# Branch A's query blocks and the output stage's pairs taken from last to first

## The chip, the cores and the metric

The kernel runs on one core of a Trainium2 chip. The metric is the device time of one execution in microseconds (us), taken on that core; lower is better. The engines are called as the profile calls them: PE (TensorE, with PEld for its weight loads), DVE (VectorE), ACT (ScalarE), POOL (GpSimd) and SP (the queue that issues every DMA of this kernel).

## The reference

One layer over 2048 tokens of width 1024. A layer norm and one wide input projection feed three branches. Branch A is sparse attention: an indexer scores all keys, each query keeps the best 256 that its 64-token chunk limit allows, and eight heads of width 64 attend to one shared key and value head. Branch B is differential attention, branch C attends to 256 memory tokens. Each branch is gated, projected to 1024 and merged; an output projection and a second layer norm end the layer.

```
h = _layer_norm(x, ln_in_g, ln_in_b)
proj = h @ w_in[l]
...
o_a = _dsa_attention(a_q, a_k, a_v, i_q, i_k, i_w).reshape(bsz, seq, A_WIDTH)
y_a = (o_a * jax.nn.silu(a_gate)) @ w_proj_a[l]
...
merged = g[:, :, 0] * y_a + g[:, :, 1] * y_b + g[:, :, 2] * y_c
h = _layer_norm(DEEPNORM_ALPHA * h + merged @ w_out[l], ln_g[l], ln_b[l])
```

Block b of branch A holds the 128 queries from token 128b on and looks at the first (b+1)*128 keys, so its work grows with b from 1 unit to 16 units of 128 keys.

## The kernel before

The 2048 tokens are 16 blocks of 128, or 8 pairs of 256. Products in float32 are made of two halves (a rounded high part and the rest), so most projections are three matmuls (`mm3`, L72 to L74). What one stage leaves for another goes through DRAM: `oa_d[b]` (branch A's result of a block), `ob_d[b]`, `mg_d[p]` (the merged sum of a pair), `tm_d`, `sg_d` (the gates), `bias_d[b]` (which keys a query of block b keeps).

A scheduler turns the program into one fixed list of instructions for each engine: an instruction goes where its operands are expected to be ready, and among those that are ready the one written first is preferred. So stages that are written one after the other are interleaved. The text below concerns the last 1000 us, in which these run beside each other:

- `attn_a(b)` (L736 to L794), branch A. For two heads at a time (a "chain" below, four for each block): the logits `lg` on PE in pieces of 512 keys (L623, L624), their eviction to `AP` on DVE (L626), the row minimum `anm` (L766), the exponential on ACT in pieces of 1024 keys (L769), then for each 256 keys a transposition `apt` on PE (L777), the split into two halves `apr` on ACT and DVE (L66, L69) and the products `aops` on PE (L782). `os`, `ot` and `ao` collect a block, which is stored to `oa_d[b]` (L794). The bias of a block has one buffer. The blocks run in an order that is written out by hand: 7, 0, 6, 1, 5, 2, 4, 3, then 8 to 15.
- `dense_g(1)`, the last of the input projection (`dps`), still under way when branch A begins.
- the loop over the pairs of branches B and C (L911 to L923): transpositions and small attention in `cps`, projections in `yps`, and the merged sum stored to `mg_d[p]` (L923). Its weights `w_proj_b` and `w_proj_c` are loaded and split first (L822, ACT L66, DVE L69, tiles `whP`).
- `stage1(p)` (L933 to L944): the gated result of branch A of a pair (`fo`, transposed in `gT`) is projected with `w_proj_a` (`yps` again, 4 pieces of 24 matmuls), multiplied by its gate `ft` on DVE (L845) and added to the sum read back from `mg_d[p]` in `facc` (L944).
- the loop over the first `EARLY` = 4 pairs (L950 to L958): `stage1`, and the sum back to `mg_d[p]` (L954). After the second of them all of `w_out` is loaded, 16 pieces of 256 KB, each split into tiles `whP` and `wwo`. These pieces and the sums take their buffers from one ring of three, named `facc`:

```
acc = accs(fs, 3)
stage1(p, acc)
...
wo += load_w(fw, fs, "facc", w_out, 4, ("wo2", "wo3"), 3)
```

- `ready(p)` (L972 to L985) fetches the sum of a pair (from DRAM for the early ones, through `stage1` for the others) and splits it into `fmT`; `stage2(b)` (L987 to L1007) multiplies by `w_out` (`fz`, PE), adds `h` and does the last layer norm. The buffers of these two lie where branch A's were, so they are free when branch A's last block is stored. The last block that runs has its norm cut finer.

Of the kernel before, what the change touches and what calls it, by code (L numbers as in the profile page):

```python
# [22 lines left out]
NB = S // 128  # L23
NP = NB // 2
# [10 lines left out]
GV = 3  # L35
AHEAD = 1
EARLY = 4
WO = (1, 1)
YT = 8
YO = 1  # L40
# [13 lines left out]
def tile_layer(ctx, tc, x, mem, ln_in_g, ln_in_b, w_in, w_mem_kv, diff_lambda, diff_norm_g,  # L54
# [589 lines left out]
    for hd in range(4):  # L644
# [25 lines left out]
        for b in order:  # L670
# [8 lines left out]
            for c in range(2):  # L679
                if b < 8 and c == 1:  # L680
                    p = both[:, 1]
                elif b < 8:
                    both = bp.tile([128, 2, 1024], F32, name="P", bufs=PB)
                    p = both[:, 0]
                else:
                    p = bp.tile([128, S], F32, name="P", bufs=PB)
# [106 lines left out]
            V.tensor_tensor(oo, oo, rc[:, 4 * h4:4 * h4 + 4, None].to_broadcast([128, 4, 64]), op=ALU.mult)  # L793
        SP.dma_start(oa_d[b], o.rearrange("p h d -> p (h d)"))  # L794

    for b in [7, 0, 6, 1, 5, 2, 4, 3, 8, 9, 10, 11, 12, 13, 14, 15]:
        attn_a(b)

    dense_g(1)
# [146 lines left out]
    def accs(ap, bufs):  # L946
        return [ap.tile([128, 2, 256], F32, name="facc", bufs=bufs) for _ in range(4)]

    wo = []
    for p in range(EARLY):  # L950
        acc = accs(fs, 3)
        stage1(p, acc)
        for u in range(4):
            SP.dma_start(mg_d[p][:, 2 * u:2 * u + 2], acc[u])  # L954
        if p == WO[0]:
            wo += load_w(hTp, fs, "facc", w_out, 0, ("hP2", "hP3"), 3)
        if p == WO[1]:
            wo += load_w(fw, fs, "facc", w_out, 4, ("wo2", "wo3"), 3)  # L958

    aps.release()  # L960
# [8 lines left out]

    MT = {}  # L970

    def ready(p):  # L972
        if p >= NP:
            return
        acc = accs(fp, 4)
        if p < EARLY:
            for u in range(4):
                SP.dma_start(acc[u], mg_d[p][:, 2 * u:2 * u + 2])
        else:
            stage1(p, acc)  # L980
        MT[p] = fp.tile([128, 2, KT, 256], F32R, name="fmT", bufs=AHEAD + 1)
        for u in range(4):
            H, L = (MT[p][:, a, 2 * u:2 * u + 2] for a in range(2))
            A.activation(H, acc[u], AF.Copy, scale=0.5)
            V.scalar_tensor_tensor(L, acc[u], 0.5, H.bitcast(F32), op0=ALU.mult, op1=ALU.subtract)  # L985

    def stage2(b):  # L987
        hh = fp.tile([128, D], F32, name="fh", bufs=3)
        SP.dma_start(hh, h_d[b])
        mT = MT[b // 2][:, :, :, 128 * (b % 2):128 * (b % 2) + 128]  # L990
        nz = 4 if b == NB - 1 else 2
        for n in range(nz):
            c = slice(n * (D // nz), (n + 1) * (D // nz))
            z = fq.tile([128, 512], F32, name="fz")[:, :D // nz]
            for k in range(KT):
                mm3(z, mT[:, 0, k], mT[:, 1, k], wo[k][:, 0, c], wo[k][:, 1, c], k == 0, k == KT - 1)
            V.scalar_tensor_tensor(hh[:, c], hh[:, c], ALPHA, z, op0=ALU.mult, op1=ALU.add)
        mu, rs = norm_stats(fp, hh, nz)
        if b < NB - 1:
            V.tensor_scalar(hh, hh, mu, rs, op0=ALU.subtract, op1=ALU.mult)  # L1000
            G.tensor_tensor(hh, hh, gln, op=ALU.mult)
            V.tensor_tensor(hh, hh, bln, op=ALU.add)
            SP.dma_start(out[b * 128:(b + 1) * 128, :], hh)
            return
        for c in (slice(0, 512), slice(512, 1024)):
            V.scalar_tensor_tensor(hh[:, c], hh[:, c], mu, gln[:, c], op0=ALU.subtract, op1=ALU.mult)
            V.scalar_tensor_tensor(hh[:, c], hh[:, c], rs, bln[:, c], op0=ALU.mult, op1=ALU.add)  # L1007
            SP.dma_start(out[b * 128:(b + 1) * 128, c], hh[:, c])

    for p in range(AHEAD):  # L1010
        ready(p)
    for p in range(NP):
        ready(p + AHEAD)
        stage2(2 * p)
        stage2(2 * p + 1)
    fq.release()
    fp.release()
    fqr.release()
# [52 lines left out]
```

## Time and profile before

| | us |
|---|---|
| median of 3 runs | 2973.35 (2971.82 to 2976.17) |
| span of the profiled execution, first to last instruction | 2965.9 |
| PE busy, PEld busy, share of the span | 95%, 92% |
| DVE, ACT, POOL busy, share of the span | 77%, 49%, 33% |
| bytes moved by DMA | 379.47 MB, mean 128 GB/s |

The runs are timed by the device around the whole execution; the span of the profile leaves out what lies before the first and behind the last instruction. The profiled execution has no time of its own in the list of runs: beside its span of 2965.9 us the median is 7.45 us longer and the fastest run 5.9 us longer. In a timeline a row gives the start, the duration, and behind the shape how many instructions of a kind are merged; what the engine waited for stands in brackets. Matmuls overlap, so the time that one costs is the distance between two starts, not its duration.

### The profile page before, as it was taken

What the parts mean: (1) busy time and instruction counts of PE and PEld (TensorE: products, weight loads), DVE (VectorE), ACT (ScalarE), POOL (GpSimd) and SP (SyncE); (2) the same over time, 40 slices, a digit from 0 to 9 for tenths busy, and PEclk for the clock granted to TensorE, in tenths of its full rate; (3) what the DMA queues carried; (4) which work ended last, traced back from release to release, by engine and by line L of the source; (5) the groups of instructions that cost most, each with busy time, mean ns of one, the idle gap of its engine ahead of it and who ended that gap; (6) DMA issues with size and microseconds to landing.
All of it is one profiled execution on the core that took longest, in us unless ns stands there. A gap on an engine that the chain in (4) does not pass through costs nothing. (4 is left out here: it accounts for less than half of the span.)

```text
span 2965.9 us, 57460 instructions
## 1 busy us (share of the span) xinstructions
PE 2830.5 (95%) x21616; PEld 2715.7 (92%) x21616; DVE 2279.2 (77%) x5309; ACT 1442.6 (49%) x2806; POOL 983.2 (33%) x1064
## 2 busy tenths in 40 slices
PE   7979998999999998999999999999999999988998
PEld 6979998999999998999999999988999999978887
DVE  6499988999899998676667766658787777776655
ACT  4345673677266772333344334446566556544100
POOL 6663547242522236323324222302222222200221
PEclk9999999999999999999999999999999999999999
DMA  6554434433232234624234242273433333256532
GB/s 208 171 191 138 159 113 156 133 119 114 94 101 76 82 93 147 201 73 140 89 118 142 77 128 80 75 242 110 133 114 119 102 113 102 86 172 224 172 131 79
DMA packets 320949, 379.47 MB, mean 128 GB/s; under 512 B 26400, under 2 KB 236832, under 8 KB 320160
## 3 DMA queue, kind: packets, MB, share of 16 engines
q1 hardware_dynamic: 320672, 375.80, 40.2%
q8 instruction: 171, 2.80, 0.4%
q14 instruction: 106, 0.87, 0.1%
HBM read 236.02 MB, written 139.69 MB: 127 GB/s over the span
## 5 line engine op out<-in xcount | busy, mean ns | idle before, releaser
L72 PE MATMUL dps<-hP,w 128*128 128x256 f32 x2048 | 582.6, 284 | 15.1 <-DVE do L69 9.9
L74 PE MATMUL dps<-hP,w 128*128 128x256 f32 x2048 | 581.7, 284 | 0.0
L73 PE MATMUL dps<-hP,w 128*128 128x256 f32 x2048 | 581.2, 284 | 0.0
L72 PE MATMUL dps<-w,hP 128*128 128x256 f32 (+1 forms) x1664 | 491.1, 296 | 12.5 <-POOL w L64 3.1
L73 PE MATMUL dps<-w,hP 128*128 128x256 f32 (+1 forms) x1664 | 490.0, 295 | 0.0
L74 PE MATMUL dps<-w,hP 128*128 128x256 f32 (+1 forms) x1664 | 487.9, 294 | 0.0
L72 PEld LDWEIGHTS dps<-hP,w 128*128 128x128 f32 x2048 | 392.6, 192 | 21.6 <-DVE do L69 10.7
L74 PEld LDWEIGHTS dps<-hP,w 128*128 128x128 f32 x2048 | 392.5, 192 | 4.4 <-POOL w L69 0.3
L73 PEld LDWEIGHTS dps<-hP,w 128*128 128x128 f32 x2048 | 392.7, 192 | 3.6
L533 ACT ACTIVATE ja<-sall,thr 128x1280 bf16<-128x1280 f32 (+4 forms) x224 | 302.2, 1349 | 122.6 <-DVE thr L529 107.1
L64 POOL TENSOR_SCALAR w<-wr 128x1024 fp32r<-128x1024 f32 x120 | 135.5, 1129 | 629.5 <-PE dps L74 404.9
L72 PEld LDWEIGHTS dps<-w,hP 128*128 128x128 f32 x1664 | 324.0, 195 | 16.8 <-issue 4.3
L69 POOL TENSOR_TENSOR w<-wr,w 128x1024 fp32r<-128x1024 f32 (+1 forms) x128 | 332.1, 2595 | 15.0 <-ACT w L66 6.9
L520 DVE TENSOR_SCALAR_CACHE_REDUCE jd<-sall,thr 128x1408 bf16<-128x1408 f32 (+6 forms) x231 | 330.9, 1433 | 5.9
L73 PEld LDWEIGHTS dps<-w,hP 128*128 128x128 f32 x1664 | 324.3, 195 | 1.8
L74 PEld LDWEIGHTS dps<-w,hP 128*128 128x128 f32 x1664 | 323.8, 195 | 2.2
L691 ACT ACTIVATE P<-P,nm 128x128 f32<-128x128 f32 (+15 forms) x128 | 154.1, 1204 | 197.8 <-DVE nm L690 187.5
L626 DVE CUSTOM_DVE_ANT_0 AP<-lg,bias 128x512 f32<-128x512 f32 (+3 forms) x304 | 181.9, 619 | 68.4 <-PE lg L624 25.1
L66 ACT CAST apr<-apt 128x512 fp32r<-128x512 f32 (+1 forms) x288 | 158.4, 563 | 141.7 <-PE apt L777 108.4
L633 DVE TENSOR_SCALAR_CACHE_REDUCE P<-lg 128x512 f32<-128x512 f32 (+3 forms) x288 | 170.4, 596 | 72.3 <-PE lg L624 71.2
L493 DVE SCALAR_TENSOR_TENSOR sall<-ir,iw,sall 128x512 f32<-128x512 f32 (+3 forms) x266 | 217.1, 865 | 8.9 <-ACT ir L489 8.0
L782 PE MATMUL aops<-apr,VA 128*128 128x256 f32 x1088 | 206.7, 297 | 16.8 <-DVE apr L69 6.7
(249 smaller groups left out, 7109.2 us busy)
## 6 DMA issues: line engine op xcount, KB each, us to landing
wr<-in_w_in_dram SPq DMA_DIRECT2D x112, 512.0 KB, 3.9
tm_d<-do SPq DMA_DIRECT2D x96, 256.0 KB, 2.1
bq<-qb_d SPq DMA_DIRECT2D x128, 128.0 KB, 3.1
aq<-qa_d SPq DMA_DIRECT2D x128, 128.0 KB, 3.1
yt<-tm_d SPq DMA_DIRECT2D x64, 256.0 KB, 3.6
sg_d<-do SPq DMA_DIRECT2D x48, 256.0 KB, 2.1
ys<-sg_d SPq DMA_DIRECT2D x48, 256.0 KB, 3.1
facc<-mg_d SPq DMA_DIRECT2D x48, 256.0 KB, 4.1
```

Of the source, the lines that this page charges most:

```text
L66: A.copy(H, src)
L69: el.tensor_tensor(L, src, H.bitcast(F32), op=ALU.subtract)
L72: PE.matmul(ps, lH, rH, start=start, stop=False)
L73: PE.matmul(ps, lH, rL, start=False, stop=False)
L74: PE.matmul(ps, lL, rH, start=False, stop=stop)
L493: V.scalar_tensor_tensor(s[:, c0:c0 + cn], r[:, :cn], iw[:, h:h + 1], s[:, c0:c0 + cn], op0=ALU.mult, op1=ALU.add)
L520: V.tensor_scalar(jd[:, :L], sc[b], t.bitcast(F32)[:, i:i + 1], None, op0=op, op1=ALU.add, accum_out=dst[:, i:i + 1])
L533: A.activation(ja[:, :L], sc[b], AF.Sign, bias=thr.bitcast(F32)[:, i:i + 1], scale=-1.0, accum_out=cnt[:, i:i + 1])
L626: V.tensor_tensor_reduce(P[:, c0:c0 + cn], ps[:, :cn], bias[:, c0:c0 + cn], scale=-0.125, scalar=-LOW, op0=ALU.add, op1=ALU.min, accum_out ...
L633: V.tensor_scalar(P[:, c0:c0 + n0], ps[:, :n0], -0.125, None, op0=ALU.mult, op1=ALU.min, accum_out=mx[:, col, nch:nch + 1])
L691: A.activation(p[:, :L], p[:, :L], AF.Exp, bias=nm[:, c:c + 1], scale=-1.0, accum_out=sm[:, c:c + 1])
L782: PE.matmul(o_ps.rearrange("p a d -> p (a d)"), VA[:, k0 + i], pr[:, a, i].rearrange("p e q -> p (e q)"), start=(k0 + i == 0 and a == 0), ...
```

## The change

Branch A takes its blocks from 15 down to 0. The early loop and the output stage take the pairs in the same order, through a table `PORD` = 7, 6, ..., 0: the first four pairs that get `stage1` early are 7, 6, 5 and 4 in place of 0 to 3, and the last block of the output stage is block 1 in place of 15. The loop of branches B and C still runs from pair 0 to pair 7. No arithmetic is added or removed, and no buffer changes size.

```
+PORD = list(range(NP - 1, -1, -1))
+LAST = 2 * PORD[-1] + 1
...
-    for b in [7, 0, 6, 1, 5, 2, 4, 3, 8, 9, 10, 11, 12, 13, 14, 15]:
+    for b in range(NB - 1, -1, -1):
         attn_a(b)
...
-    for p in range(EARLY):
+    for i in range(EARLY):
+        p = PORD[i]
...
-        if p == WO[0]:
+        if i == WO[0]:
...
-    def ready(p):
-        if p >= NP:
+    def ready(i):
+        if i >= NP:
             return
+        p = PORD[i]
         acc = accs(fp, 4)
-        if p < EARLY:
+        if i < EARLY:
...
-        nz = 4 if b == NB - 1 else 2
+        nz = 4 if b == LAST else 2
...
-        stage2(2 * p)
-        stage2(2 * p + 1)
+        stage2(2 * PORD[p])
+        stage2(2 * PORD[p] + 1)
```

On every engine the lists are the same up to the first instruction that depends on branch A's order. Lines of the new kernel are two to four higher.

**The start of branch A, on PE**, where the last input projections (`dps`) run out. Before, with block 7:

```order
L777 MATMUL apt<-idf,AP 128x128 x6
L623 MATMUL lg<-KA_15284,aq 128x512
L624 MATMUL lg<-KA_15284,aq 128x512
L72 MATMUL dps<-hP_25629,w 128x256
L73 MATMUL dps<-hP_25629,w 128x256
L74 MATMUL dps<-hP_25629,w 128x256
L623 MATMUL lg<-KA_15284,aq 128x512
L624 MATMUL lg<-KA_15284,aq 128x512
L72 MATMUL dps<-hP_25629,w 128x256
L73 MATMUL dps<-hP_25629,w 128x256
L74 MATMUL dps<-hP_25629,w 128x256
L782 MATMUL aops<-apr,VA_15286 128x256 x4
```

Now, with block 15:

```order
L76 MATMUL dps<-hP_25629,w 128x256
L625 MATMUL lg<-KA_15284,aq 128x512
L626 MATMUL lg<-KA_15284,aq 128x512
L625 MATMUL lg<-KA_15284,aq 128x512
L626 MATMUL lg<-KA_15284,aq 128x512
L625 MATMUL lg<-KA_15284,aq 128x512
L626 MATMUL lg<-KA_15284,aq 128x512
L625 MATMUL lg<-KA_15284,aq 128x512
L626 MATMUL lg<-KA_15284,aq 128x512
L779 MATMUL apt<-idf,AP 128x128 x6
```

Eight pieces of logits stand ahead of the first full set of transpositions of block 15, where block 7 had four, and the `dps` have run out by then.

**The end of the early pairs, on DVE**, around the split of the last piece of `w_out` (`wwo`). Before, inside block 15:

```order
L69 TENSOR_TENSOR apr<-apt,apr 128x512
L626 ISA AP,amx<-lg,bias 128x512
L626 ISA amx 128x1
L69 TENSOR_TENSOR wwo_34288<-facc,wwo_34288 128x512 x2
L944 TENSOR_TENSOR facc<-facc,ft 128x512
L766 TENSOR_REDUCE anm<-amx 128x1
L836 SCALAR_TENSOR_TENSOR yoT<-gT,yoT 128x4x128
L69 TENSOR_TENSOR apr<-apt,apr 128x512
L830 TENSOR_TENSOR fo<-fo,ys 128x512
L944 TENSOR_TENSOR facc<-facc,ft 128x512
L69 TENSOR_TENSOR apr<-apt,apr 128x512
L845 SCALAR_TENSOR_TENSOR ft<-ft,yps 128x512
```

Now:

```order
L71 TENSOR_TENSOR wwo_34288<-facc,wwo_34288 128x512
L795 TENSOR_TENSOR ao<-ao,arc 128x256
L71 TENSOR_TENSOR wwo_34288<-facc,wwo_34288 128x512
L832 TENSOR_TENSOR fo<-fo,ys 128x512
L838 SCALAR_TENSOR_TENSOR yoT<-gT,yoT 128x4x128
L946 TENSOR_TENSOR facc<-facc,ft 128x512 x2
L838 SCALAR_TENSOR_TENSOR yoT<-gT,yoT 128x4x128
L832 TENSOR_TENSOR fo<-fo,ys 128x512
L847 SCALAR_TENSOR_TENSOR ft<-ft,yps 128x512 x2
L946 TENSOR_TENSOR facc<-facc,ft 128x512
L989 SCALAR_TENSOR_TENSOR fmT<-facc,fmT 128x512 x4
```

Branch A's last result (`ao`) now stands ahead of the last split, no eviction or split of branch A is left behind it, and the output stage's `fmT` follows at once.

**The same place on SP.** Before (`mg_d_274` is pair 3, the fourth early one, `oa_d_254` block 15, `mg_d_271` pair 0):

```order
L954 DMA mg_d_274<-facc 128x512
L941 DMA ft<-tm_d_4_219 128x512
L829 DMA ys<-sg_d_6_197 128x512
L794 DMA oa_d_254<-ao 128x512
L966 DMA gln<-in_ln_g_dram 128x1024
L968 DMA bln<-in_ln_b_dram 128x1024
L978 DMA facc<-mg_d_271 128x512 x4
```

Now (`mg_d_276` is pair 5, the third early one, `oa_d_239` block 0, `mg_d_278` pair 7):

```order
L944 DMA facc<-mg_d_276 128x512 x2
L796 DMA oa_d_239<-ao 128x512
L944 DMA facc<-mg_d_276 128x512
L939 DMA fo<-oa_d_243 128x512
L831 DMA ys<-sg_d_2_193 128x512
L969 DMA gln<-in_ln_g_dram 128x1024
L943 DMA ft<-tm_d_5_220 128x512 x2
L957 DMA mg_d_276<-facc 128x512 x2
L971 DMA bln<-in_ln_b_dram 128x1024
L982 DMA facc<-mg_d_278 128x512 x4
```

The last store of branch A and the output stage's first loads now stand in the middle of the early pairs, where they stood behind all four.

## Rows read from the trace of the kernel before

**Rows 1.** Busy time by stretch, from the start of branch A on

```profile
core 0: us, PE busy (x) PEld busy (x) DVE busy (x) ACT busy (x) POOL busy (x), PEclk, DMA share, GB/s
1956.00:2010.00 54.00, 46.69 (x325) 42.24 (x324) 39.72 (x113) 34.69 (x78) 4.38 (x4) 0.94 0.83 258
2010.00:2163.00 153.00, 147.60 (x1142) 138.57 (x1141) 121.83 (x394) 94.91 (x244) 36.26 (x36) 1.00 0.47 132
2163.00:2592.00 429.00, 423.51 (x3292) 402.52 (x3291) 323.56 (x879) 256.05 (x588) 103.45 (x103) 1.00 0.34 102
2592.00:2613.60 21.60, 17.85 (x120) 14.73 (x119) 17.48 (x42) 14.37 (x29) 1.65 (x1) 1.00 0.70 230
2613.60:2740.00 126.40, 113.52 (x871) 107.87 (x870) 88.03 (x176) 53.47 (x98) 0.00 (x0) 0.97 0.60 187
2740.00:2958.00 218.00, 218.00 (x1120) 184.41 (x1120) 124.74 (x181) 20.66 (x35) 48.08 (x45) 0.99 0.39 134
...
2740.00:2760.00 20.00, 20.00 (x76) 16.00 (x77) 10.55 (x17) 4.10 (x7) 1.57 (x3) 0.87 0.65 235
```

**Rows 2.** The timeline of PE in places without a wait

```profile
2610.38 0.60 PE L777 MATMUL apt<-idf,AP 128*128 128x128 f32 x4
2610.74 0.48 PE L623 MATMUL lg<-KA,aq 128*128 128x512 f32 x1
...
2618.50 0.28 PE L74 MATMUL yps<-yoT,whP 128*128 128x256 f32 x1
2618.62 0.64 PE L782 MATMUL aops<-apr,VA 128*128 128x256 f32 x4
2619.10 0.38 PE L777 MATMUL apt<-idf,AP 128*128 128x128 f32 x2
...
2628.74 0.39 PE L623 MATMUL lg<-KA,aq 128*128 128x512 f32 x1
2628.97 0.40 PE L624 MATMUL lg<-KA,aq 128*128 128x512 f32 x1
```

**Rows 3.** Groups of PE from 2613.5 to 2739.8: line, operation, count, busy, mean ns, idle

```profile
L73 PE MATMUL yps<-yoT,whP 128*128 128x256 f32 x160 | 46.9, 293 | 0.0
...
L782 PE MATMUL aops<-apr,VA 128*128 128x256 f32 x149 | 29.8, 303 | 8.2 <-ACT apr L66 4.1 <-DVE apr L69 4.0
L777 PE MATMUL apt<-idf,AP 128*128 128x128 f32 x142 | 21.9, 277 | 0.0
```

**Rows 4.** The timeline of SP: the first and the last loads of w_out

```profile
2657.30 0.33 SPq L822 DMA_DIRECT2D facc<-in_w_out_dram  x1
...
2676.99 11.43 SPq L822 DMA_DIRECT2D facc<-in_w_out_dram  x8
```

**Rows 5.** The timeline of DVE in the early pairs

```profile
2648.86 0.68 DVE L845 SCALAR_TENSOR_TENSOR ft<-ft,yps 128x512 f32<-128x512 f32 x1
...
2691.42 1.29 DVE L69 TENSOR_TENSOR wwo<-facc,wwo 128x512 fp32r<-128x512 f32 x2
...
2698.42 0.69 DVE L944 TENSOR_TENSOR facc<-facc,ft 128x512 f32<-128x512 f32 x1 [2.57 <-DMA facc<-mg_d]
...
2699.67 0.69 DVE L845 SCALAR_TENSOR_TENSOR ft<-ft,yps 128x512 f32<-128x512 f32 x1
```

**Rows 6.** The timeline of PE at the end of the w_out loads

```profile
2699.77 0.63 PE L782 MATMUL aops<-apr,VA 128*128 128x256 f32 x3 [3.98 <-DVE apr L69]
...
2700.60 0.44 PE L72 MATMUL yps<-yoT,whP 128*128 128x256 f32 x1
```

**Rows 7.** The start of branch A: DVE, then ACT by form, then PE

```profile
1958.87 0.69 DVE L626 CUSTOM_DVE_ANT_0 AP<-lg,bias 128x512 f32<-128x512 f32 x1 [16.23 <-DMA bias<-bias_d]
1959.49 0.08 DVE L626 DVE_READ_ACCUMULATOR2_ANT amx<- 128x1 f32 x1
...
L769 ACT ACTIVATE AP<-AP,anm 128x1024 f32<-128x1024 f32 x80 | 92.3, 1154 | 26.0 <-DVE anm L766 25.7
...
1999.43 1.11 PE L833 MATMUL cps<-idf,yo 128*128 128x128 f32 x4 [3.54 <-POOL yo L830]
```

More of the change, by code (lines that the diff above doesn't have):

```diff
@@ L954, in tile_layer @@
             SP.dma_start(mg_d[p][:, 2 * u:2 * u + 2], acc[u])
-        if p == WO[0]:
+        if i == WO[0]:
             wo += load_w(hTp, fs, "facc", w_out, 0, ("hP2", "hP3"), 3)
-        if p == WO[1]:
+        if i == WO[1]:
             wo += load_w(fw, fs, "facc", w_out, 4, ("wo2", "wo3"), 3)
@@ L998, in stage2 @@
         mu, rs = norm_stats(fp, hh, nz)
-        if b < NB - 1:
+        if b != LAST:
             V.tensor_scalar(hh, hh, mu, rs, op0=ALU.subtract, op1=ALU.mult)
```

## The prediction

> **What bounds the kernel now.** I read the busy times by stretch first, then the timeline of PE for what each kind of matmul costs, then the timelines of SP, DVE and PE where a stretch loses time. PE bounds nearly all of the last 1000 us: from 2163 to 2592 it is busy for 423.5 of 429 us, and no other engine comes near (DVE 323.6) [rows 1]. The change does not touch that work, it only deals it out anew. So the question is where PE stands still, and whether the new order stands still less. The reader is to see three places in rows 1: the start of branch A (1956 to 2010: PE busy 46.7 of 54 us, granted clock 0.94), the stretch with small blocks of branch A (2010 to 2163), and the stretch of block 15 and the early pairs (2613.6 to 2740: 113.5 of 126.4 us, clock 0.97). From 2740 to 2958 PE never stops.
>
> Matmuls overlap, so I price them from start to start [rows 2]: 0.12 us for 256 columns (`yps`, and `aops` at 0.48 for four), 0.36 for four transpositions, 0.23 for 512 columns of logits. The stretch from 2613.6 to 2740 has 480 `yps` and 149 `aops`, so 75.5 us, 142 `apt` [rows 3] and, counted in the order, 52 other transpositions, 17.5 us, and 46 logits, 10.6 us: 103.6 us of work in 126.4. It loses 22.8.
>
> The Trainium skill (Perfetto Trace Analysis, Identifying the Most-Contended Engine) says that matmul busy time is a poor measure of what is left to gain and weight-load busy time a better one. Here the first leaves 12.9 us and the second 18.5 [rows 1], so by the page more is to be had than the busy row tells; my count of 22.8 goes its way.
>
> **The start of branch A.** Its first two heads need eight evictions and four exponentials before their transpositions can run, where block 7 needed four and two. An eviction takes 0.62 us from start to start and an exponential 1.15 [rows 7], so 4 x 0.62 + 2 x 1.15 = 4.8 us later. The `dps` that covered block 7's first steps are the same number and have run out by then. Against it stands that before, PE waits 3.5 us for the first operands of branch B, with block 7 and the tiny block 0 as its only other work [rows 7], and block 15 has more to put there. The bias of block 15 has twice the bytes of block 7's, and DVE already waited 16.2 us for that one, while PE had `dps` [rows 7]. Ends: 5 us lost, 4 us gained. I take 3 us lost, nearer to the first, because the missing evictions are certain and the wait is one.
>
> **The loop of branches B and C.** Each block has four chains, and each chain begins with a stretch in which only logits can run. With small blocks beside the loop (2010 to 2163, some 28 chains) the weight loads leave 14.4 us open, or 0.5 us for each chain; with big ones (2163 to 2592, also 28) 26.5 us, or 0.95 [rows 1]. Before, 60 chains stand beside the loop (15 blocks); now the loop lasts until the middle of block 3, about 49. Eleven chains at 0.5 to 0.95 are 5 to 10 us. They are not gone, they come back beside the early pairs. Ends: 0, if they lose as much there, and 8 gained, if they lose nothing. I take 3 gained, nearer to 0, because what those early pairs have to offer as cover is itself short of work (next).
>
> **Between the loop and the early pairs** PE has 21.6 us with only branch A, while `w_proj_a` is split and the first gate is formed [rows 1]. The same steps stand there now, with 11.5 us of branch A's work where there were 12.2: 0. The first early pair is now pair 7, whose sum the loop has only just stored, but the sum is wanted some 6 us after the first projection and is loaded well before it; covered by that projection: 0.
>
> **The early pairs.** This is the term that decides. Before, block 15 fills PE while `w_out` comes in; now blocks 2, 1 and 0 are all that is left, and by the order 61.4 us of work stand between the first early projection and the first `fz` (336 `yps`, 56 `aops`, 112 transpositions, 40 narrow logits) in place of 103.6. So 42.2 us of work leave this stretch and are done earlier, beside the loop. If the stretch could shrink by as much, nothing is lost or won. But it holds a chain of its own, the ring of three buffers that the sums and the 16 pieces of `w_out` share:
> - From the first early projection (2613.6) until DVE takes the second piece of the second pair 35.3 us pass [rows 5]. PE's work up to there is 32 us before and 28 to 30 now, so I take 33.
> - From there to the first load of `w_out` 8.4 us [rows 4], the sum being stored and its buffer freed: kept.
> - The 16 loads and splits. Before they run from 2657.3 to 2692 [rows 4, 5], 35 us, the first half held up by branch A's instructions on ACT and DVE. The last eight were issued in 11.4 us, 1.43 each [rows 4]. Sixteen at that pace are 23, and with about 4 for the last one to land and be split 27.
> - From the last split to the next projection of PE, the first of the fourth pair: 2692 to 2700.6, 8.6 us, since DVE first waits for a sum to be read back [rows 5, 6]. Kept.
> - Two pieces of `yps` ahead of the first `fz`, 48 x 0.12 = 5.8.
>
> The sum is 33 + 8.4 + 27 + 8.6 + 5.8 = 82.8 us, and 126.4 - 82.8 = 43.6 us shorter against 42.2 us of work moved out: 1.4 us gained, so 1. The stretch is then no longer full of work, it waits: 82.8 - 61.4 = 21.4 us, as much as it lost before. Ends: with the second piece reached 5 us earlier and loads at 23 us 9 to 10 gained; with 35.3 and 35 us kept 8.6 to 9 lost.
>
> **The output stage** has the same work in pairs and loses nothing [rows 1]; its last block is cut finer as before: 0.
>
> **Sum.** +3 - 3 - 1 = -1 us against the profiled span of 2965.9: 2964.9. The median of the runs is 7.45 us above that span, so **2972 us**. A measurement of this kernel can tell about 0.2% (6 us) from no change.
>
> **Rivals.**
> - *The tail really empties.* The eleven small chains hide wholly in the time in which PE waits for `w_out` anyway (8 gained), the ring starts earlier because PE reaches the second pair sooner and less stands in its way (6 gained), and the start costs nothing. For it: 21 us of waiting are room enough for 11 chains of under 1 us. Against it: the ring starts with the same two pairs, and PE's work ahead of it is hardly less. 14 us off: 2959.
> - *`w_out` loses its cover* (the other side). The place is the ring of early pairs: its loads take 35 us as before and start as late, and PE, in its fixed order, stands before the first projection of the fourth pair with nothing else to do. Price: 2.3 us and 8 us from the two steps of the ring (35.3 for 33, 35 for 27), less the 1.4 gained, so 9; then the clock, which after the waits of this stretch is granted at 0.87 from 2740 to 2760 [rows 1], 2.6 us of lost work, 3 more if the longer wait adds as much again; and the start's 3. In all 15 us: 2988. It decides when more than about 30 us lie between the first and the last load of `w_out`. For it: PE already waited 4.0 us just there, with block 15 at hand [rows 6]. Against it: ACT and DVE have less of branch A between the loads.
>  The Trainium skill (TensorE: Matmul & The Clock Gate, HAM oscillation — how this bites in real kernels) has the rule that speaks against the change: a gap in which PE waits for DMA puts its clock back to half rate, so that the work behind it starts cold. The trace agrees as far as it goes, with 0.87 behind the waits [rows 1]; it would make the price above the rule and not the exception.
> - *The change is not what it says*: the lists show the blocks from 15 to 0 and the pairs from 7 to 0, so this has no chance of its own.
>
> **How the numbers follow.** The forecast, losses that move without changing, has 0.40; the emptied tail 0.35; `w_out` without cover 0.25. The first covers about 2966 to 2979, and the sum's ends reach from 4 + 8 + 10 = 22 gained to 5 + 9 = 14 lost, with 3 to 5 more for the clock. All ends at once are unlikely; leaving out a tenth on each side the range is 2956 to 2988. Faster by over 0.2% is the second case, 0.35, slower the third, 0.25, the same 0.40.
>
> **What would show it.** The first transpositions of block 15 come about 5 us later after the start of branch A than block 7's. The loop of B and C ends later than 2592 by about the work moved, some 20 to 25 us. About 83 us lie between the first projection of the early pairs and the first `fz`, with a wait of PE of 10 us or more, released by DVE, behind the last split of `w_out`, and a lower granted clock after it. I am wrong if that wait is missing (then the tail empties), if the loads of `w_out` take 35 us or more, or if the loop of B and C runs longer than its work.

## The result: 0.95% slower

The changed kernel takes 2999.1 us (median of 4 runs, 2995.0 to 3005.9), the kernel before 2972.6 in the same comparison (2971.6 to 2976.2). The ratio is 1.0095, with a 95% interval of 1.0075 to 1.0114: 26.5 us lost between the medians. The forecast was 2972 and its range ended at 2988. The side was that of the rival in which `w_out` loses its cover, but both the size and the cause are others.

The profiled execution of the changed kernel lasts 3005.85 us, with a span of 3004.1. Its first logits of branch A come 11.9 us later than before (1967.7 against 1955.9), although the lists are identical up to there. The change has no part in this: in the 20 profiled executions of this study that point lies anywhere from 1955.1 to 1967.7. From there to PE's last matmul pass 1002.1 us before and 1028.4 now, 26.3 more, which is nearly the difference of the medians; all that follows is about this part.

The busy time by stretch of the kernel before, cut at the places where the program changes its stage (start of branch A to the first merged sum stored; loop of branches B and C; between; early pairs; output stage). Columns as in [rows 1]:

```profile
core 0: us, PE busy (x) PEld busy (x) DVE busy (x) ACT busy (x) POOL busy (x), PEclk, DMA share, GB/s
1955.86:2073.10 117.24, 107.10 (x777) 97.34 (x776) 93.99 (x301) 77.40 (x187) 16.64 (x17) 0.97 0.60 179
2073.10:2599.00 525.90, 516.64 (x4019) 490.99 (x4018) 397.85 (x1101) 313.27 (x731) 129.07 (x127) 1.00 0.37 111
2599.00:2613.60 14.60, 12.05 (x81) 9.87 (x80) 10.75 (x28) 9.48 (x19) 0.03 (x1) 1.00 0.75 254
2613.60:2739.80 126.20, 113.32 (x871) 107.67 (x869) 87.83 (x176) 53.27 (x98) 0.00 (x0) 0.97 0.60 187
2739.80:2958.00 218.20, 218.20 (x1120) 184.61 (x1120) 124.94 (x181) 20.86 (x35) 48.08 (x45) 0.99 0.39 134
```

The same of the changed kernel, with two rows at its end: 20 us near the end of the early pairs, and a stretch in their middle:

```profile
1967.70:2094.00 126.30, 115.57 (x795) 104.67 (x795) 93.03 (x238) 78.80 (x160) 18.44 (x19) 0.95 0.43 138
2094.00:2651.20 557.20, 541.73 (x4171) 509.16 (x4171) 416.24 (x1132) 325.96 (x744) 126.14 (x125) 1.00 0.35 105
2651.20:2665.80 14.60, 12.95 (x87) 10.15 (x87) 12.44 (x38) 9.89 (x26) 0.00 (x0) 1.00 0.93 268
2665.80:2762.80 97.00, 76.81 (x546) 72.24 (x545) 65.45 (x185) 39.83 (x106) 0.00 (x0) 0.84 0.73 237
2762.80:2996.20 233.40, 233.40 (x1270) 200.34 (x1268) 129.37 (x191) 20.62 (x34) 48.10 (x45) 1.00 0.42 141
2740.00:2760.00 20.00, 9.08 (x42) 7.83 (x43) 11.27 (x19) 5.21 (x9) 0.00 (x0) 0.58 0.91 313
2716.10:2726.40 10.30, 8.85 (x35) 7.28 (x36) 7.56 (x22) 5.22 (x16) 0.00 (x0) 0.50 0.84 265
```

Busy rows hide part of the idling, so I did what the prediction did in one place for the whole stretch: every matmul of PE's timeline is priced from start to start (0.233 us for 512 columns, 0.175 for 384, 0.119 for 256, 0.0875 for 128; [rows 2] show three of these to two digits), and what passes beyond the price is called **loss**. From the first logits of branch A on both traces hold the same 6859 matmuls, so the work so priced is 900.5 us in both kernels. It is only dealt out anew, and the loss is the whole result (the expectations further down name losses from a rougher count, about 2 us lower in the loop):

| us | work before | loss before | work now | loss now |
|---|---|---|---|---|
| start of branch A | 91.9 | 25.3 | 99.5 | 26.7 |
| loop of B and C | 481.6 | 44.4 | 498.0 | 59.2 |
| between | 9.7 | 4.9 | 9.5 | 5.1 |
| early pairs, to the first `fz` | 102.5 | 23.6 | 61.1 | 35.9 |
| output stage | 214.9 | 3.4 | 232.3 | 1.1 |
| all | 900.5 | 101.7 | 900.5 | 128.0 |

Two stages make the difference: the loop loses 14.8 us more, the early pairs 12.3.

**The early pairs.** The three largest waits of PE in this stretch of the changed kernel: engine, what waits, for what, us in total, times, the longest:

```profile
PE gT L835 <- DVE yoT L838: 6.1, 3, 3.0
PE aops L784 <- ACT os L787: 4.4, 1, 4.4
PE gT L835 <- DVE fo L832: 3.8, 1, 3.8
```

From its last 25 us: PE's timeline, the issues on SP, two steps on DVE, and the split of the first sum on ACT:

```profile
2739.87 0.66 PE L790 MATMUL ot<-idf,os 128*128 128x128 f32 x4 [1.49 <-ACT os L787]
2742.96 0.69 PE L835 MATMUL gT<-idf,fo 128*128 128x128 f32 x4 [2.43 <-DVE yoT L838]
2746.63 1.12 PE L835 MATMUL gT<-idf,fo 128*128 128x128 f32 x4 [2.98 <-DVE yoT L838]
2751.59 1.09 PE L835 MATMUL gT<-idf,fo 128*128 128x128 f32 x4 [3.84 <-DVE fo L832]
2754.35 0.55 PE L74 MATMUL yps<-yoT,whP 128*128 128x256 f32 x1 [1.67 <-DVE ft L847]
2754.70 0.42 PE L75 MATMUL yps<-yoT,whP 128*128 128x256 f32 x1
2754.91 0.42 PE L76 MATMUL yps<-yoT,whP 128*128 128x256 f32 x1
```

```profile
2711.63 0.33 SPq L824 DMA_DIRECT2D facc<-in_w_out_dram  x1
...
2736.93 3.70 SPq L824 DMA_DIRECT2D facc<-in_w_out_dram  x3
...
2743.85 0.38 SPq L796 DMA_DIRECT2D oa_d<-ao  x1
...
2750.56 3.19 SPq L982 DMA_DIRECT2D facc<-mg_d  x4
```

```profile
2750.75 0.69 DVE L832 TENSOR_TENSOR fo<-fo,ys 128x512 f32<-128x512 f32 x1 [1.62 <-DMA ys<-sg_d]
2753.51 1.33 DVE L847 SCALAR_TENSOR_TENSOR ft<-ft,yps 128x512 f32<-128x512 f32 x2 [2.07 <-DMA ft<-tm_d]
```

```profile
2758.18 2.49 ACT L988 ACTIVATE fmT<-facc 128x512 fp32r<-128x512 f32 x4 [9.79 <-DMA facc<-mg_d]
```

Block 0, one unit of work, ends branch A at 2743.85; the last piece of `w_out` was issued 3 us earlier; and behind `ot`, PE has only gate transpositions that follow one another through DVE, with nothing between them. Where such steps stand in [rows 6] there are projections or block 15 beside them. DVE is in turn held by loads: 5.3 us of its waits from 2744 to 2754 end with one, the two longest shown above. The clock granted from 2740 to 2760 is 0.58, and the `yps` behind the waits start 0.21 us apart until 2760, where [rows 2] have 0.12. In this stretch it had been 0.50 before, from 2716.1 to 2726.4 and shortly at 2692.

A part of the loss is therefore the clock's. At 0.50 a matmul costs up to about twice its price (projections start 0.21 us apart for 0.12, transpositions at 1988 0.21 for 0.11), so the work done there costs at most its price once more: 3.7 us from 2716.1 on, 4.0 from 2743.4 to 2760.5 and 1.7 at 2692, against 3.2 in two short places of the same stretch before. By this estimate up to 6 of the 12.3 us are the clock's; the other 6 or more are waiting. Before, the first 5 us of the output stage were at half rate too, with 3.0 us of work; now none of it is, which accounts for the 2.3 us by which that stage is better.

**The loop.** Here no wait is long: the longest of PE is 1.7 us. I cut the loop into windows of 4 us and asked how much of each is projections (`yps`). Before, 46 windows have less than 0.8 us of them and lose 25.3 us together; now 54, and they lose 42.8. All other windows lose 17.8 before and 15.6 now. So the extra loss lies where only branch A and the small attention steps of B and C stand. Eight more windows of the old sort (0.55 us each) would be 4.4 us; the greater part is that such a window now loses 0.79. Two stretches of the changed loop show the difference, the first almost without projections:

```profile
2380.00:2400.00 20.00, 17.05 (x113) 13.94 (x111) 14.53 (x41) 12.94 (x32) 4.51 (x5) 1.00 0.28 81
...
2420.00:2440.00 20.00, 20.00 (x161) 19.41 (x160) 14.70 (x42) 13.08 (x35) 4.74 (x6) 1.00 0.40 123
```

And the group of the projections (the first of the three lines of `mm3`) in the one and in the other, 3 against 24:

```profile
L74 PE MATMUL yps<-yoT,whP 128*128 128x256 f32 x3 | 0.9, 316 | 0.0
...
L74 PE MATMUL yps<-yoT,whP 128*128 128x256 f32 x24 | 6.8, 285 | 0.0
```

The waits of PE that the profile shows in the loop grew from 8.5 to 14.4 us, some 6 of the 14.8. What grew are branch A's own steps, logits behind an eviction and products behind a split (before, then now):

```profile
PE lg L623 <- DVE amx L626: 1.2, 3, 0.6
PE aops L782 <- DVE apr L69: 0.9, 3, 0.3
PE aops L782 <- ACT apr L66: 0.7, 2, 0.6
```

```profile
PE lg L625 <- DVE amx L628: 4.0, 6, 1.7
PE aops L784 <- ACT apr L68: 3.1, 5, 1.1
PE aops L784 <- DVE apr L71: 2.3, 8, 0.3
```

The rest is spacing beyond the price that the list of waits does not show. This loss is no chance. The pair of the loop that holds the first of these stretches loses 11.8 us here, and 11.1 to 12.0 in the six other kernels below that share this part of the list.

### The profile page after: what moved, and what is told of

Its sections match the earlier page's. It is cut to its first block, busy times and chain, and to the rows that moved or that the text cites. A ratio compares the mean times of both kernels' runs of the same rounds, so it can differ in the third digit from the quotient of the medians.

```text
span 3004.1 us, 57468 instructions
## 1 busy us (share of the span) xinstructions
PE 2845.0 (95%) x21616; PEld 2723.4 (91%) x21616; DVE 2291.2 (76%) x5309; ACT 1443.2 (48%) x2806; POOL 984.5 (33%) x1064
## 5 line engine op out<-in xcount | busy, mean ns | idle before, releaser
L74 PE MATMUL dps<-w,hP 128*128 128x256 f32 (+1 forms) x1664 | 490.3, 295 | 11.8 <-POOL w L66 3.1
L74 PEld LDWEIGHTS dps<-hP,w 128*128 128x128 f32 x2048 | 392.5, 192 | 27.9 <-DVE do L71 13.5
L71 DVE TENSOR_TENSOR apr<-apt,apr 128x512 fp32r<-128x512 f32 (+1 forms) x288 | 185.0, 656 | 57.2 <-ACT apr L68 55.2
L74 PE MATMUL yps<-yoT,whP 128*128 128x256 f32 x768 | 222.9, 292 | 2.0 <-DVE ft L847 1.7
## 6 DMA issues: line engine op xcount, KB each, us to landing
bq<-qb_d SPq DMA_DIRECT2D x128, 128.0 KB, 3.0
aq<-qa_d SPq DMA_DIRECT2D x128, 128.0 KB, 3.0
```

What stands on the lines that cost most here:

```text
L71: el.tensor_tensor(L, src, H.bitcast(F32), op=ALU.subtract)
L74: PE.matmul(ps, lH, rH, start=start, stop=False)
```

## The experiments

Each run is timed beside the kernel before on its own chip, so the ratios compare. The table has the order of the blocks, the loss by stage worked out as above ("early" with "between"), and the ratio. `alt` stands for 7, 0, 6, 1, 5, 2, 4, 3.

| run | blocks | start | loop | early | output | all | ratio (95%) |
|---|---|---|---|---|---|---|---|
| before | alt, 8 to 15 | 25.3 | 44.4 | 28.5 | 3.4 | 101.7 | 1 |
| changed | 15 to 0 | 26.7 | 59.2 | 41.0 | 1.1 | 128.0 | 1.0095 (1.0075 to 1.0114) |
| e1 | 14 to 0, 15 | 20.4 | 54.5 | 52.6 | 2.6 | 130.2 | 1.0114 (1.0089 to 1.0140) |
| e2 | 7 to 4, 8 to 15, 3 to 0 | 24.2 | 53.3 | 47.7 | 1.1 | 126.3 | 1.0093 (1.0064 to 1.0122) |
| e3 | 15 to 0, ring of 4 | 24.2 | 61.7 | 37.1 | 1.1 | 124.1 | 1.0088 (1.0065 to 1.0112) |
| e4 | 15 to 0, w_out first | 25.1 | 61.0 | 41.2 | 1.0 | 128.3 | 1.0105 (1.0080 to 1.0130) |
| e5 | as before, early pairs 3 to 0 | 24.3 | 43.5 | 25.2 | 2.3 | 95.4 | 1.0001 (0.9987 to 1.0015) |
| e6 | alt, 15 to 8 | 22.3 | 50.7 | 34.0 | 1.1 | 108.1 | 1.0029 (1.0015 to 1.0042) |
| e7 | 0 to 15 | 36.8 | 55.7 | 30.1 | 1.1 | 123.7 | 1.0080 (1.0061 to 1.0099) |
| e8 | as before, ring of 4 | 25.7 | 44.5 | 27.1 | 3.6 | 101.0 | 1.0007 (0.9992 to 1.0023) |
| e9 | 15 to 8, alt | 24.7 | 61.9 | 33.7 | 3.8 | 124.0 | 1.0065 (1.0045 to 1.0086) |
| e10 | 15 to 2 | 24.7 | 60.0 | 24.6 | 12.5 | 121.8 | 1.0038 (1.0025 to 1.0050) |
| e11 | as before without 0, 1 | 21.5 | 51.1 | 31.3 | 1.1 | 105.0 | 0.9987 (0.9971 to 1.0004) |
| e12 | 15, 0, 14, 1 ... 8, 7 | 27.9 | 50.5 | 40.3 | 2.1 | 120.8 | 1.0054 (1.0037 to 1.0070) |
| e13 | 7, 0, 8, 1 ... 13, 6, 14, 15 | 23.6 | 50.1 | 25.1 | 1.1 | 99.8 | 0.9992 (0.9978 to 1.0006) |
| e14 | alt, 14 to 8, 15 | 22.3 | 58.4 | 28.0 | 1.2 | 109.9 | 1.0034 (1.0022 to 1.0047) |
| e15 | 15 to 2, w_out first | 25.3 | 62.1 | 33.8 | 1.4 | 122.6 | 1.0046 (1.0023 to 1.0068) |
| e16 | as before, w_out first | 24.6 | 44.0 | 39.2 | 2.6 | 110.4 | 1.0026 (1.0009 to 1.0042) |
| e17 | 15 to 0, two gate buffers | 25.3 | 59.6 | 44.4 | 1.1 | 130.4 | 1.0097 (1.0071 to 1.0123) |
| e18 | as before, two gate buffers | 27.4 | 43.0 | 33.6 | 3.5 | 107.5 | 1.0016 (1.0002 to 1.0030) |

Work is 900.5 us in all but the runs without blocks 0 and 1 (890.9). The loss is that of one execution and tells the ratio to within some 7 us: the three kernels with the blocks as before and a ratio near 1 (before, e5, e8) have 95 to 102.

### Is it the tail, or the order as such?

e1 puts block 15 last, e2 leaves the loop with ascending blocks and puts only 3 to 0 last.

```
-PORD = list(range(NP - 1, -1, -1))
+PORD = [6, 5, 4, 3, 2, 1, 0, 7]
-    for b in range(NB - 1, -1, -1):
+    for b in [14, 13, 12, 11, 10, 9, 8, 7, 6, 5, 4, 3, 2, 1, 0, 15]:
```

```
-    for b in range(NB - 1, -1, -1):
+    for b in [7, 6, 5, 4, 8, 9, 10, 11, 12, 13, 14, 15, 3, 2, 1, 0]:
```

> Blocks 14 to 0, then block 15 last; pairs 6 to 0, then 7. By the order 45 us of branch A stand again between the first early projection and the first fz (42 in the kernel before, 18 in the changed one), while the loop of branches B and C runs beside descending blocks as in the changed kernel. Theory 'tail' (time is lost where PE has no branch A left while w_out is loaded): PE's loss between first early projection and first fz falls from 35.7 to about 23 us, the loop keeps its 57 us of loss, 2986 us in all, half of the way back. Theory 'all tail' (the loop's extra loss of 14 us is chance of one execution): 2973. Rival 'descending order alone' (blocks that shrink are at fault everywhere): 2995 or more.

> The converse: 7, 6, 5, 4, then 8 to 15 ascending beside the loop, then 3, 2, 1, 0; pairs from 7 to 0. By the order 16 us of branch A stand in the stretch of the early pairs, as few as in the changed kernel (18). Theory 'tail' with a loop of its own cost: the early pairs lose about 36 us as in the changed kernel, the loop about 43 as before, 2986 us in all. Theory 'descending order alone': 2973. Theory 'all tail': 2999.

They contradict each other by these theories. e1 has more of branch A in the early pairs than the kernel before, and still loses more there than the changed kernel (52.6 us with "between", which alone has 14.0 for 4.9); its 1.0114 fits "descending order alone" only. e2 keeps the big blocks ascending and is as slow as the changed kernel, 1.0093, which by its size fits "all tail" only; but its loop loses 53.3 us for 44.4, which that theory has no place for. So a big block at the end is not enough, and ascending big blocks neither. The stores of e2's blocks 15, 3, 2, 1, 0 on SP show what both have in common:

```profile
2642.74 0.38 SPq L796 DMA_DIRECT2D oa_d<-ao  x1
...
2659.98 0.33 SPq L796 DMA_DIRECT2D oa_d<-ao  x1
...
2688.22 1.53 SPq L796 DMA_DIRECT2D oa_d<-ao  x1
...
2710.76 0.33 SPq L796 DMA_DIRECT2D oa_d<-ao  x1
...
2730.25 0.43 SPq L796 DMA_DIRECT2D oa_d<-ao  x1
```

Blocks of 4, 3, 2 and 1 units take 17, 28, 23 and 19 us: from store to store, small blocks next to each other take some 20 us, and not in proportion to their work. In the kernel before the stores of blocks 0 and 1 follow 16.0 and 12.4 us behind those of blocks 7 and 6 (2014.31 to 2030.34, 2058.61 to 2071.05).

### The ring, `w_out` and the gates

e3 and e8 give the ring a fourth buffer, in the changed kernel and in the one before. e4 and e16 load `w_out` one pair earlier. e17 and e18 give the gates of the early pairs two buffers.

```
-        acc = accs(fs, 3)
+        acc = accs(fs, 4)
...
-            wo += load_w(fw, fs, "facc", w_out, 4, ("wo2", "wo3"), 3)
+            wo += load_w(fw, fs, "facc", w_out, 4, ("wo2", "wo3"), 4)
```

```
-WO = (1, 1)
+WO = (0, 0)
```

```
-            gated(fs, fqr, "gT", o, fs.tile([128, 512], F32, name="ys", bufs=1), 0, b, V, oT)
+            gated(fs, fqr, "gT", o, fs.tile([128, 512], F32, name="ys", bufs=2), 0, b, V, oT)
```

> The changed kernel with four buffers in place of three in the ring of the early sums and the raw pieces of w_out. If the ring paces the 16 loads (28.7 us from the first issue to the last) and PE waits for them, the loads take some 20 to 24 us and the kernel gains 4 to 8 us over the changed one: 2991 to 2995. Rival (the splits on ACT and DVE, or the sums ahead of them, set the pace): under 2 us, 2997 to 3000.

> The kernel before with four buffers in the ring of the early sums and w_out. In the changed kernel a fourth buffer took 8 us of loss out of the stretch from the first early projection to the first fz. If the ring holds PE up here as well, the 22.7 us lost in that stretch fall by 3 to 8 and the ratio is 0.997 to 0.999. Rival (block 15 covers the loads, the ring costs nothing): 1.000 within 0.001.

> The changed kernel with w_out loaded behind the first early pair instead of the second. If the stretch is bound by a chain that begins with the first load of w_out (2711.6 in the changed kernel) and PE merely waits at its end, the first load moves some 20 us ahead, into the time of blocks 2 and 1, and 8 to 13 us come back: 2986 to 2991. Rival (what PE lacks is work, wherever the loads stand, since the pairs behind them wait for the same ring): 2997 to 3002.

> The kernel before with w_out loaded behind the first early pair. The prediction took the ring of w_out for what sets the stretch of the early pairs. If that holds here, the wait of 4 us behind the last split goes and the ratio is 0.997 to 0.999. If the small and late steps of branch A set it and the ring is beside them: 1.000 within 0.0015.

> The changed kernel with two buffers in place of one for the gates of the early pairs (ys). In the changed kernel PE waits 9.9 us in that stretch before gate transpositions, and DVE waits for ys up to 1.6 us at a time. If the chain of gates sets the end, the loss between first early projection and first fz falls from 35.7 by 5 to 9 us, ratio to the kernel before 1.006 to 1.008. Rival (small blocks and w_out end as late, the gates only stand in line behind them): 1.009 to 1.0105.

> The same in the kernel before. If the gates' single buffer holds PE there too (it waits 2 to 3.4 us before gate transpositions around the early pairs), the ratio is 0.998 to 0.9995, and this is a version faster than both. Rival (block 15 fills those waits): 1.000 within 0.001.

e3 takes 8 us out of the early pairs (27.6 lost for 35.9) and gives 6 of it back ahead of them (between 9.5 for 5.1, last pair of the loop 11.4 for 9.8); 1.0088 cannot be told from 1.0095. e8 gains nothing. e4 is the test of the prediction's ring. Its first and last `w_out` issues on SP, and its early pairs:

```profile
2676.06 1.86 SPq L824 DMA_DIRECT2D facc<-in_w_out_dram  x2
...
2708.71 1.70 SPq L824 DMA_DIRECT2D facc<-in_w_out_dram  x2
```

```profile
2657.30:2759.20 101.90, 83.65 (x595) 79.10 (x594) 67.03 (x189) 38.15 (x104) 0.00 (x0) 0.88 0.78 244
```

The loads are through 49 us ahead of the first `fz`, where the changed kernel has 22, and nothing is won: 1.0105. In the kernel before the same edit costs 0.26%, all of it in the early pairs. The gates are no cause either: e17 is where the changed kernel is, e18 slightly slower than before. So the rivals of e3, e8 and e17 held; e4's held in its sense, though 1.0105 is some 3004 us and its range ended at 3002; e16 and e18 came out slower than either of their ranges, e18 with an interval that reaches into its rival's. Neither ring nor weights nor gates alone end the stretch, though PE waits for each of them.

One rival is left untested. In e4 DVE waits in the early pairs for the loads that feed a piece:

```profile
DVE ft L847 <- DMA ft<-tm_d: 12.8, 6, 3.4
```

In the changed kernel that row has 2.1 us and the gates' loads 5.7. By the busy times above, the changed stretch moves nearly the bytes that it moved before (237 GB/s for 97.0 us are 23.0 MB, 187 for 126.2 are 23.6) in 29 us less. Whether these loads come late because of the traffic beside them, no run shows.

### The pairs' order

```
+PORD = [3, 2, 1, 0, 4, 5, 6, 7]
```

> The kernel before, with branch A's old order, but the early pairs (and the first pairs of the output stage) taken as 3, 2, 1, 0 in place of 0, 1, 2, 3. It tells what the order of the pairs costs by itself. Theory 'branch A' (the order of the blocks makes the loss, the pairs only follow): the ratio to the kernel before is 1.000 within 0.002. Rival 'pairs' (the sums and gates come back at another time, which stalls the ring): 1.004 or more.

1.0001: taking the early pairs in reverse costs no more than the interval allows, 0.15%. For all eight pairs this wasn't tried, since pairs 7 to 4 can't go first before blocks 8 to 15 are done.

### The order of the blocks, piece by piece

In this order e6, e9, e7, e12, e13 and e14; where no `PORD` stands, e9 takes the pairs from 7 to 0, e7 and e13 from 0 to 7.

```
+PORD = [0, 1, 2, 3, 7, 6, 5, 4]
+    for b in [7, 0, 6, 1, 5, 2, 4, 3, 15, 14, 13, 12, 11, 10, 9, 8]:
...
+    for b in [15, 14, 13, 12, 11, 10, 9, 8, 7, 0, 6, 1, 5, 2, 4, 3]:
...
+    for b in range(NB):
...
+PORD = [7, 0, 6, 1, 5, 2, 4, 3]
+    for b in [15, 0, 14, 1, 13, 2, 12, 3, 11, 4, 10, 5, 9, 6, 8, 7]:
...
+    for b in [7, 0, 8, 1, 9, 2, 10, 3, 11, 4, 12, 5, 13, 6, 14, 15]:
...
+PORD = [0, 1, 2, 3, 6, 5, 4, 7]
+    for b in [7, 0, 6, 1, 5, 2, 4, 3, 14, 13, 12, 11, 10, 9, 8, 15]:
```

> The small blocks first and alternating as before (7, 0, 6, 1, 5, 2, 4, 3), the big ones from 15 down to 8; pairs 0 to 3, then 7 to 4. Descending order is left in, but the small blocks stand again at the beginning. Theory 'small blocks late' (the loss comes where blocks 7 to 0 run beside the end of the loop and the early pairs, with too little between their steps): the loop loses some 43 to 46 us of PE as before, ratio 1.000 to 1.004. Rival 'every other list' (the loss depends on where block ends meet the steps of branches B and C, and the old order happened to fit): loop over 50 us, ratio 1.006 or more.

> The changed kernel with only the last eight blocks in another order: 15 to 8 descending, then 7, 0, 6, 1, 5, 2, 4, 3, so that each very small block stands beside a bigger one; pairs from 7 to 0 as in the changed kernel. Theory 'serial small blocks' (a block of 1 to 4 units takes some 20 us however little work it has, because its four chains follow each other; beside a bigger block that time is filled, next to another small one it isn't): PE's loss in loop, early pairs and between falls by 8 to 15 us against the changed kernel, ratio to the kernel before 1.004 to 1.007. Rival 'late, whatever their order' (small blocks at the end lack the projections of the loop): 1.008 to 1.011 as in the changed kernel.

> Blocks 0 to 15 in their natural order, pairs as before. The small blocks stand at the beginning but don't alternate with bigger ones, the big ones as before. 'Small blocks late': start of branch A a few us worse (blocks 0 to 3 give PE next to nothing beside the first steps), the rest as before, ratio 1.000 to 1.004. 'Every other list': loss in the loop over 50 us too, ratio 1.006 or more.

> Every small block beside a big one from the start: 15, 0, 14, 1, 13, 2, 12, 3, 11, 4, 10, 5, 9, 6, 8, 7, pairs 7, 0, 6, 1, 5, 2, 4, 3. Descending big blocks, and 49 us of branch A in the stretch of the early pairs (42 before). 'Serial small blocks': the loop and the early pairs lose as little as before or less, ratio 0.996 to 1.002. Rival 'descending big blocks cost' (as the 8.6 us of the run with 15 down to 8): 1.003 to 1.006. Rival 'every other list': 1.008 or more.

> Small blocks beside big ones as in the run that spread them downwards (ratio 1.0054), but the big ones ascending: 7, 0, 8, 1, 9, 2, 10, 3, 11, 4, 12, 5, 13, 6, 14, 15, pairs as before. 'Descending big blocks cost': gone with the descent, ratio 0.998 to 1.002. Rival 'every other list' (the old order merely fits, and spreading is no help): 1.004 or more.

> As the run with the big blocks from 15 down to 8 (ratio 1.0029), but block 15 last: 7, 0, 6, 1, 5, 2, 4, 3, 14 to 8, 15; pairs 0 to 3, 6, 5, 4, 7. If the size of the last block is what those 8.6 us were: 1.000 within 0.0015. If the descent beside the loop costs (its loop lost 49 us where before lost 43): 1.002 to 1.004.

e6 and e9 cut the change into three steps, in us of 2968: turning only the big blocks round costs 0.29%, 8.6 us; moving the alternating small ones behind them 0.36% more, 10.7 us; ending their alternation (the changed kernel) 0.30% more, 8.9 us. The first two intervals don't touch; the last two overlap a little (1.0075 to 1.0086), so the third step is the least certain. The intervals leave the steps uncertain by 4, 7 and 8 us, and the losses give 6.4, 15.9 and 4.0. With the second step the early pairs turn round as well, since they have to follow the blocks. e6's ratio is in the range of "small blocks late", its loop, 50.7 us, is not; e9's is in that of "serial small blocks", but loop, between and early pairs together lose only 4.6 us less than in the changed kernel, where 8 to 15 were expected.

e7 was missed by "small blocks late": with the small ones at the beginning but in a row, the start loses 36.8 us for 25.3 and the loop 55.7 for 44.4, 22 us more in all. Place alone is not it, then; neighbours matter. e13 and e12 show what the old order has: e13 is another order with every small block beside a bigger one and the sizes rising, and it is as fast as before (0.9992). "Every other list is worse" is refuted for the whole time, but not for the loop: the five kernels with the old list of blocks lose 43.0 to 44.5 us there, every other list 50 or more, e13 50.1. e13 makes it up in the other stages. With the bigger blocks falling (e12) it costs 0.54%, as the rival of descending blocks said, and e14 shows that this is not the size of the last block: with 15 last, descending big blocks still cost 0.34%, beside the loop (58.4 lost for 44.4, and in the windows with few projections 40.8 for 25.3).

### What the smallest blocks cost

```
     def attn_a(b):
         L = (b + 1) * 128
+        if b < 2:
+            o = apl.tile([128, 8, 64], F32, name="ao", bufs=1)
+            G.memset(o, 0.0)
+            SP.dma_start(oa_d[b], o.rearrange("p h d -> p (h d)"))
+            return
```

> The changed kernel without the attention of blocks 0 and 1: their result is stored as zeros. By the order 9.6 us of PE's work fall out (at the price of a matmul from start to start). 'Serial small blocks': in the changed kernel these two blocks take 43 us at the end of the early pairs, and PE has too little else there; leaving them out saves 20 to 30 us, ratio 1.000 to 1.003. Rival 'work only' (the tail waits for something else, such as w_out or the sums): about 10 us, ratio 1.006.

> The kernel before without the attention of blocks 0 and 1 (zeros stored): 9.8 us of PE's work fall out. 'Serial small blocks': beside blocks 7, 6 and 5 their time is filled, so leaving them out saves little more than their work, 8 to 14 us, ratio 0.995 to 0.997. Rival (tiny blocks cost their 20 us anywhere): 25 us or more, ratio 0.992 or less.

> The changed kernel without the attention of blocks 0 and 1 (zeros stored), and w_out loaded behind the first early pair. Without these blocks alone the first fz came at 2718 us, while w_out's last piece was issued at 2737, and the output stage then lost 12.5 us in place of 1.1. Theory 'two chains' (the small blocks end last in the changed kernel, w_out's loads stand right behind them): with the loads some 20 us earlier too, the output stage loses 1 to 4 us, ratio 1.000 to 1.001 where it was 1.0038. Rival (the loss moves into the early pairs, where the sums wait for the same ring): 1.003 to 1.005.

e10 saves 0.57% against the changed kernel, 17 us for 9.6 us of work, between both theories. e11 saves 0.13%, 4 us for as much work, less than either of its theories had, and its interval reaches to no gain at all: its loop, with another list, loses 51.1 us for 44.4. The difference of 13 us (give or take 9, from the intervals) is what the place and the neighbours of these two blocks make in these two lists. In e10 the first `fz` is reached 34 us sooner after the start of branch A, and then PE stands in the output stage for the next one that is late:

```profile
2731.32 0.65 PE L74 MATMUL fz<-wwo,fmT 128*128 128x512 f32 x1 [2.32 <-ACT wwo L68]
```

That looked like a second chain just behind the first. e15 moves `w_out` ahead of it, and the output stage does lose only 1.4 us; but the early pairs then lose 28.4 us for 18.0, and the ratio is 1.0046. The rival held: in this stretch loss moves from one wait to the next.

## Why the prediction was wrong

**The start of branch A** (+3, ends -4 and +5). The first full set of transpositions comes 13.1 us after the first logits before (1968.95) and 19.9 now (1987.58): 6.8 us later for the forecast 5, and DVE waits 16.6 us for the bias where [rows 7] have 16.2. But the loss up to the first stored sum grew by only 1.4 us, and the six other kernels with this start have 24.2 to 25.3. The delay was right; its price was nearer 0.

**The loop of B and C** (-3, ends 0 and -8): measured +14.8. This is the step that failed first. I gave a chain a fixed price of 0.5 to 0.95 us by the weight loads of two stretches and multiplied by eleven chains fewer. The runs show no fixed price: with fewer chains the loop loses a third more, 59.2 us for 44.4, in the windows in which no projection stands beside the chain, and each such window loses more than before. The sign named in the prediction came out: the last projection of the loop falls 51.0 us later, 39 of them behind the same start, of which 24.9 are the work moved ahead of it and the rest loss.

**Between** (0): 0.2. **The output stage** (0): 2.3 us better, by the clock. The prediction had the work that leaves the early pairs done earlier, beside the loop; of the 41.4 us only 23.9 went ahead of them, 17.4 went behind the first `fz`. Its own counts say so, 480 `yps` and then 336: 144 of them, 17.1 us, only come later. The sum does not depend on it.

**The early pairs** (-1, ends -10 and +9): the second step that failed. The work was right (61.1 us, forecast 61.4), the time was 97.0 for 82.8, so +12.3 in loss for a forecast of -1. Second piece of the second pair 36.9 us after the first projection (forecast 33, as in [rows 5] 35.3); from there to the first load of `w_out` 8.9 (8.4); from it to the end of the last split 32.7 (27, in [rows 4, 5] 35); from there to the first `fz` 18.5 (14.4). Every step came out longer than forecast, and those of the second piece and of the loads nearer to their old values. The 27 us rested on the pace of the last eight loads (read as 1.43 us each; 11.43 us are seven steps and one issue, so nearer 1.6, and sixteen nearer 25 than 23); the sixteen loads of the changed kernel took 29 us to issue, and why is not shown. And the sum treated the ring as the chain that sets the end. e4, e15 and e16 refute that: with the loads 20 to 27 us sooner the stretch loses as much or more, and e3's fourth buffer shortens it only to lose most of that ahead of it.

**The rival on the other side** named 15 us and asked for more than 30 us between the first and last load of `w_out`: there are 29 to the issue of the last, 33 to its split. Its size for the tail was right (9 and 3 to 6 for the clock against 12.3), its cause, the loads of `w_out`, was not, so this is luck as far as the 9 go. The sign I asked for, waits behind the last split and a lower clock, is there: 8.5 us released by DVE at 2746 to 2754, and 0.58.

**What was shown and what stays open.** Shown: the order of the early pairs, the ring, the loads of `w_out` and the gates are not the cause, each taken by itself; the order of branch A's blocks is, in steps of about 9, 11 and 9 us. Small blocks are dear beside other small blocks or at the end, and cost nothing that can be measured beside a bigger one with sizes rising. Not shown: by which instructions big blocks in descending order lose in the loop. That the loss sits in windows short of projections tells where it is, not why: in e13, which is not slower, they lose 33.4 us for 25.3, and in e12, 0.54% slower, only 27.6. Why the scheduler places the projections so is not known. A second bias buffer, against DVE's waits at block ends (2.8 us in the loop), was not tried, nor the loads beside the early pairs, nor more than one of ring, weights and gates at a time. No version with all its work was clearly faster than the kernel before.

## What to carry to other kernels

When the work of a bound engine is only dealt out anew, ask at each moment whether it has a long independent job to fill with, and not only how many chains need one: here fewer chains lost more. For the order of unequal pieces, these runs speak for the smallest each beside a bigger one, with the sizes rising towards the end; how far this holds for another kernel, they do not say. A wait that stands last in a timeline need not be the bound: move its source ahead and see whether the end moves.

## What the runs showed of the hardware

The first 1956 us, the same list of instructions on PE in all 20 profiles, varied by 12.6 us, almost half of the effect that was looked for, and by 8.0 us on one and the same chip (e5 to e8); so stages are to be compared from their own start.

The clock fell further behind waits than I had taken: to 0.58 over 20 us with PE busy for 9.1 of them, and to 0.50 over 10.3 us with PE busy for 8.9, the latter from the end of a wait of 4.4 us for ACT on; the 0.87 of [rows 1] stands where PE is busy throughout. At 0.50 (1.2 GHz for 2.4) a projection matmul started every 0.21 us in place of 0.12. The rule of the Trainium skill that was weighed in the prediction (TensorE: Matmul & The Clock Gate, HAM oscillation — how this bites in real kernels) agrees with that, though the page tells it of waits for DMA. The price is no small part of the stretch: by the estimate above up to 6 of its 12.3 us.

Four loads of sums issued from 2750.56 on were first used at 2758.18, 7.6 us later; from 2740 to 2760 the DMA engines were busy for 0.91 of the time at 313 GB/s.
